# Conditioning chunks that hold a quarter of all four column blocks, and another order of the SSD outputs, in a hybrid decoder block

## The chip, the cores and the metric

The kernel runs on one core of one Trainium2 chip. The metric is the device time of one launch in microseconds (us), the median of three runs. One core has a matrix engine (PE, with its weight loads shown apart as PEld), three engines for elementwise work (DVE, ACT, POOL) and a queue of its own for transfers (SP); they run side by side, each in the order of its own instruction stream, and wait for one another through semaphores.

## The reference

One layer of a decoder for 256 prompt tokens and 8 samples of 4 tokens, 288 token columns in all. A conditioning vector per request (1 prompt + 8 samples, 9 columns) gives six modulation vectors of 2048; the layer is a modulated norm, one input projection shared by a pooling mixer and a Mamba-2 SSD mixer, one output projection, and a gated MLP with a short causal convolution.

```python
def block(x, c, st_pool, st_conv, st_ssm, st_ffn, pos0, lp):
    mod = silu(c) @ lp['w_ada'] + lp['b_ada']                 # 2048 -> 6 * 2048
    sh1, sc1, g1, sh2, sc2, g2 = split(mod, 6)
    h = rmsnorm(x, lp['norm1']) * (1 + sc1) + sh1
    u_pool, z, xbc, dt_raw = split(h @ lp['w_in'], [512, 2048, 4608])
    pool_out, new_pool = pool_mixer(u_pool, st_pool, pos0, lp['pool_w'], lp['pool_scale'])
    ssd_out, new_conv, new_ssm = ssd_mixer(z, xbc, dt_raw, st_conv, st_ssm, ...)
    x = x + g1 * (concatenate([pool_out, ssd_out]) @ lp['w_out'])
    h2 = rmsnorm(x, lp['norm2']) * (1 + sc2) + sh2
    gate, val = split(h2 @ lp['w_up'], 2)                     # 2 * 5504 wide
    gate_c, new_ffn = causal_dwconv(gate, st_ffn, ...)        # width 3
    return x + g2 * ((silu(gate_c) * val) @ lp['w_down'])

def ssd_chunked(xdt, dA, Bm, Cm, h0):                         # chunks of 128 tokens
    cs = cumsum(dA)
    y_diag = einsum(Cm, Bm, exp(cs_l - cs_s) masked, xdt)     # within a chunk
    y_off = einsum(Cm, h_start, exp(cs))                      # from the state at its start
    return y_diag + y_off, h_final
```

The last norm and the new states are outputs too. The six modulation vectors are the conditioning "parts" 0 to 5 (shift, scale and gate of the mixer, then of the MLP).

## The kernel before

Weights are streamed through SP's queue in chunks of 128 partitions by 1024 numbers (512 KB), by `load` (L209 to L212), into a pool of eight slots with the tag "raw"; a ninth is added in the output projection. A chunk of a projection is split by `split` into a rounded high part (ACT, L217) and the rest (DVE, L218), and each 128 x 128 block of it makes three matmuls with 288 columns (`mm3`, L223 to L225: high by high, high by low, low by high). They make up most of the work of PE. The matmuls on f32 operands, as the conditioning has them, leave two rows each in the trace.

Stages, in order of time: parts 0 and 1 of the conditioning in groups (`ada_group_units`, matmuls named adag), which gate the first modulation; the projection to x, B and C of the SSD mixer (xbc) and to its time steps (dt); the projections to z and to the pooling input (uz); the output projection (out, 16 blocks m); the second norm; the up projection in gate and value blocks (`up_pair`), the first three pairs with the weights upk in one sweep; the down projection and the last norm.

Parts 2 to 5 are not needed at once. `ada_part_units` (L312) makes one as a generator that other loops pull: it loads chunks, multiplies them, and yields after each visit. For a part there are 16 blocks k of 128 rows, and for each k two chunks h. Chunk h holds the column blocks j = 2h and 2h + 1 of the part, 512 columns each. `ada_mm` (L252) multiplies a chunk's block j with the stationary operand `sc_c[:, k, :]` (the nine conditioning columns after SiLU, padded to 32) and puts the result into rows 32j to 32j + 31 of one PSUM tile, so the four blocks use four column groups of the PE array. A visit is `AY` = 2 blocks k, so 4 chunks and 8 matmuls, in the order in which the chunks were loaded. When all k are in, ACT copies the tile (`asb`, L257), PE transposes it in four blocks of 128 columns (L263), and four additions on DVE (L327) put the result with the bias into `ada`.

Parts 2, 3 and 4 form one chain (`adas`). It is pulled in the last section of xbc (RA1), in the uz loop (RA2), once after it (TA) and after each block m of the output projection. Part 5 has visits of one k (default `ay=1`): GA = (2, 3), two before and three after the sums of the second norm (`final_sum`), and then two for each pair from the fourth on in `up_pair`'s loop.

The SSD mixer goes through four groups g of six heads, three turns t of two heads each. In a turn `decays(t)` broadcasts the cumulated log decays of two heads by a PE matmul each (cse, L682), ACT makes relu and exp (L687 to L689), DVE multiplies e by C·B (L690), and POOL multiplies ec by C (L691). One turn later `outputs(t)` makes the turn's ten matmuls: the samples' state part (yo by a selector, L700) and the samples' own (L703), 32 columns wide, the first prompt chunk (L706), and the second, which has a part from its own tokens (xdt1 by e, L709) and one from the state before it (s1 by ec, L710), 128 wide. Each has two row halves of 64, one for each head. The result goes to DVE, ACT (square) and POOL (sum of squares). All these stages are generators too, pulled between the matmuls of the uz loop (`pull(back, ...)`), as are those of the pooling mixer (`pool_units`, its matmul at L770).

The order on each engine is the compiler's: it cuts and interleaves the visits and the turns with the main stream of `mm3`.

Of the kernel before, what the change touches and what calls it, by code (L numbers as in the profile page):

```python
# [11 lines left out]
F32 = mybir.dt.float32  # L12
F32R = mybir.dt.float32r
AF = mybir.ActivationFunctionType
ALU = mybir.AluOpType
PSUM = bass.MemoryType.PSUM

P = 128
# [26 lines left out]
RA1, RA2, RB1, RB2, RB3 = 0.5, 0.4, 1.0, 1.0, 1.0  # L45
TA, ADA_OUT = 4, 4
TK = 4
GA = (2, 3)
XM = (0, 2, 5, 9)
SM0 = 10  # L50
YC = [(0, 1), (1, 1)] + [(m, 2) for m in range(2, KT, 2)]
# [80 lines left out]
def kernel(ctx: ExitStack, tc, ins, outs):  # L132
# [29 lines left out]
    ada = kp.tile([P, 6, KT, NC9], F32, name="ada")  # L162
    amul = kp.tile([P, 2, KT, NC9], F32, name="amul")
    bada = early[:, V_BADA:V_BADA + 96].rearrange("p (a k) -> p a k", a=6)
    sc_c = kp.tile([P, KT, 32], F32, name="sc_c")
    nc.vector.memset(sc_c, 0.0)
    nc.scalar.activation(sc_c[:, :, 0:NC9], ct, AF.Silu)

    wps = aux("warm")

# [37 lines left out]
    def load(key):  # L208
        off, cols = S.items[key]  # L209
        t = wp[0].tile([P, RAWC], F32, tag="raw", name="raw_" + "_".join(map(str, key)))  # L210
        nc.sync.dma_start(t[:, :cols], wflat[off:off + P * cols].rearrange("(p n) -> p n", p=P))
        return t  # L212
# [36 lines left out]
    def ada_mm(ps, raw, k, c0, nb, js):  # L249
        for j in js:  # L250
            c = c0 + (j - js[0]) * nb
            nc.tensor.matmul(ps[32 * j:32 * j + 32, :nb], sc_c[:, k, :], raw[:, c:c + nb],  # L252
                             start=(k == 0), stop=(k == KT - 1), tile_position=(0, 32 * j))

    def ada_sb(ps, nb, name, r=P):
# [16 lines left out]
    def ada_group_units(gi):  # L272

        k0, gk = KGROUPS[gi]
        nj = min(2 * gk, 4)
        nb = 2 * gk * P // nj
        per = RAWC // (nj * nb)
        ps = pa.tile([P, 512], F32, tag="ada", name=f"adag{gi}")
        for q in range(KT // per):
            raw = load(("ada", gi, q))  # L280
            yield
            if gk == 1:

                for kk in range(0, per, 2):
                    k = q * per + kk
                    for j in range(4):
                        nc.tensor.matmul(ps[32 * j:32 * j + 32, :nb], sc_c[:, k + j // 2, :],
                                         raw[:, kk * 256 + j * P:kk * 256 + j * P + P],
                                         start=(k == 0), stop=(k == KT - 2), tile_position=(0, 32 * j))
                if gi == 0 and q < WU[3]:  # L290
                    warm_pe(WU[2], raw[:, 0:P])
                continue
            for kk in range(per):
                ada_mm(ps, raw, q * per + kk, kk * nj * nb, nb, range(nj))
        r = 32 * nj
        if gk == 1:
            asb = ada_sb(ps, nb, f"g{gi}")
            pt = aux(f"adat_g{gi}")
            nc.tensor.matmul(pt[:, :r], asb[:, :nb], early[:, K_S2:K_S2 + r], start=True, stop=True)
            if gi == 0:  # L300
                warm_pe(WU[4], asb[:, 0:P])
        else:
            pt = ada_tr(ada_sb(ps, nb, f"g{gi}", r), nb, f"g{gi}", r)
        for i in range(nb // P):

            o = ada[:, 0:2, k0:k0 + gk, :].rearrange("p a (b i) c -> p a b i c", b=nj // 2)[:, :, :, i, :]
            b = bada[:, 0:2, k0:k0 + gk].rearrange("p a (b i) -> p a b i", b=nj // 2)[:, :, :, i]
            src = pt[:, i * r:(i + 1) * r].rearrange("p (a b c) -> p a b c", a=2, b=nj // 2)[:, :, :, 0:NC9]
            nc.vector.tensor_tensor(o, src, b.unsqueeze(3).to_broadcast([P, 2, nj // 2, NC9]), ALU.add)
        ada_scale(0, 1, early[:, V_N1:V_N1 + KT], k0, gk)  # L310

    def ada_part_units(part, ay=1):  # L312
        ps = pa.tile([P, 512], F32, tag="ada", name=f"adap{part}")
        for k in range(KT):
            raws = [load(("adap", part, k, h)) for h in range(2)]
            for h in range(2):
                ada_mm(ps, raws[h], k, 0, 512, range(2 * h, 2 * h + 2))
            if k % ay == ay - 1:
                yield
        asb = ada_sb(ps, 512, f"p{part}")  # L320
        yield
        pt = ada_tr(asb, 512, f"p{part}")
        for i in range(4):
            o = ada[:, part].rearrange("p (j i) c -> p j i c", j=4)[:, :, i, :]
            b = bada[:, part].rearrange("p (j i) -> p j i", j=4)[:, :, i]
            src = pt[:, i * P:(i + 1) * P].rearrange("p (j c) -> p j c", j=4)[:, :, 0:NC9]
            nc.vector.tensor_tensor(o, src, b.unsqueeze(2).to_broadcast([P, 4, NC9]), ALU.add)  # L327
        if part == 4:
            ada_scale(1, 4, vec[:, V_N2:V_N2 + KT], 0, KT)
        yield  # L330
# [56 lines left out]

    nc.scalar.activation(warm, sc_c[:, 0, 0:1], AF.Sqrt, scale=0.0)  # L390
    warm_pe(WU[0])
    ssum = aux("ssum1")
    for q in range(4):
# [12 lines left out]
    col_sums(ssum, sqs, early[:, K_S4:K_S4 + 1], True, True)  # L406
    rstd1p, rstd1 = rstd_of(ssum, D, "rstd1")

    cvp = [mx.tile([P, 5, CW], F32, tag="cvp", name=f"cvp{g}", bufs=4) for g in range(4)]

    def cvs(g):
# [189 lines left out]
    def ssd_group(g):  # L601
# [92 lines left out]
        def outputs(t, e, ec):  # L694
            assert (g, t) in zdone
            pq = aux(f"y{g}_{t}")
            rows = [slice(0, 64), slice(64, P)]
            for i, r in enumerate(rows):
                f = slice(64 * (2 * t + i), 64 * (2 * t + i) + 64)
                nc.tensor.matmul(pq[r, NP:N], yo[:, f], seli, start=True, stop=False)  # L700
            for i, r in enumerate(rows):
                f = slice(64 * (2 * t + i), 64 * (2 * t + i) + 64)
                nc.tensor.matmul(pq[r, NP:N], xdt[:, 2, f], e[:, i, NP:N], start=False, stop=True)  # L703
            for i, r in enumerate(rows):
                f = slice(64 * (2 * t + i), 64 * (2 * t + i) + 64)
                nc.tensor.matmul(pq[r, 0:P], xdt[:, 0, f], e[:, i, 0:P], start=True, stop=True)  # L706
            for i, r in enumerate(rows):
                f = slice(64 * (2 * t + i), 64 * (2 * t + i) + 64)
                nc.tensor.matmul(pq[r, P:NP], xdt[:, 1, f], e[:, i, P:NP], start=True, stop=False)  # L709
                nc.tensor.matmul(pq[r, P:NP], s1[:, f], ec[:, i, :], start=False, stop=True)  # L710
            yt = cf[:, t, 0:N]
            nc.vector.scalar_tensor_tensor(out=yt, in0=yt,
                                           scalar=vec[:, V_D + 3 * g + t:V_D + 3 * g + t + 1],
                                           in1=pq[:, :N], op0=ALU.mult, op1=ALU.add)
            zt = zy[g][:, t, :]
            nc.vector.tensor_tensor(zt, zt, yt, ALU.mult)
            sq = kp.tile([P, N], F32, tag="xsq", name=f"ysq{g}_{t}", bufs=2)
            nc.scalar.activation(sq, zt, AF.Square)
            if g + t == 0:
                nc.gpsimd.tensor_copy(ssq, sq)  # L720
            else:
                nc.gpsimd.tensor_tensor(ssq, ssq, sq, ALU.add)
# [249 lines left out]
            drain(adas)  # L972


    adag2 = ada_part_units(5)
    for k in range(2):
        ready[("upk", k)] = split(load(("upk", k)), 0, 2 * FK * P, f"upk{k}")
    for _ in range(GA[0]):
# [102 lines left out]
    for gi, (k0, nk) in enumerate(DGROUPS):  # L1081
        for j in range(k0, k0 + nk):
            up_pair(j)
            if gi == 0 and j >= 3:
                next(adag2, None)
                next(adag2, None)
            if j >= SM0:
                next(states, None)
            if gi and j == k0:
                drain(adag2)  # L1090
                down(gi - 1)
# [32 lines left out]
def _layout(inp):  # L1124
# [62 lines left out]
    for key in _STREAM.order:  # L1187
        o, cols = _STREAM.items[key]
        kind = key[0]
        if kind == "ada":  # L1190
            k0, gk = KGROUPS[key[1]]
            per = RAWC // (256 * gk)
            s = wa[key[2] * per:(key[2] + 1) * per, :, 0:2, k0:k0 + gk]
            s = s.transpose(1, 0, 2, 3, 4)
        elif kind == "dt":
            s = wdt.transpose(1, 0, 2)
        elif kind == "adap":
            s = wa[key[2], :, key[1], 8 * key[3]:8 * key[3] + 8]
        elif kind == "xbc":
            ks, ms = _xbc_chunks(key[1])[key[2]]  # L1200
            s = wx[ks][:, :, ms].transpose(1, 2, 0, 3)
        elif kind == "upk":
            s = wu[key[1]][:, [m for j in range(FK) for m in (j, FT + j)]]
        elif kind == "down":
            k0, nk = DGROUPS[key[1]]
            a, n = _halves(nk)[key[3]]
            s = wd[k0 + a:k0 + a + n, :, key[2]].transpose(1, 0, 2)
        else:
            mat, m0 = full[kind]
            a, n = _halves(KT)[key[-1]]  # L1210
            s = mat[a:a + n, :, m0 + key[1]].transpose(1, 0, 2)
        w[o:o + P * cols] = s.reshape(-1)
# [47 lines left out]
```

## Time and profile before

| | us |
|---|---|
| runs | 1397.7, 1397.77, 1396.01; median 1397.7 |
| profiled execution, its own time | 1395.98 |
| its span | 1394.2 |
| mean granted clock of PE | 0.997 |
| DMA, mean rate over the span | 232 GB/s |

The span is the time from the first to the last instruction of the profiled execution; its own time holds what lies around that as well. In a row of the timeline stand the start, the length, the engine, the line, the operation with its output and inputs, and how many rows it stands for; a bracket gives the idle time before it and what ended it. For matmuls the ends are modelled, and they overlap, so what a run of them takes is read from its start to the start of what follows. In a group's row the busy time and the mean of one row in nanoseconds follow the bar. Line numbers are those of the kernel before.

### The profile page before, as it was taken

To read this page: it belongs to the slowest core of one execution; us is meant where nothing else is said; L and a number is where in the kernel's file an instruction comes from. 1 tells how busy PE (TensorE), PEld (TensorE's weight loads), DVE (VectorE), ACT (ScalarE), POOL (GpSimd) and SP (SyncE) were. 2 spreads that over 40 slices of the span, in tenths; PEclk is the share of its full clock that TensorE was granted. 3 is DMA by queue.
4 is the path that set the end of the run, shared out by engine and by line. 5 is a ranking of instruction groups with operands and counts; after the bars stand their busy time and mean duration, and the time that the engine had idled before them with its cause. 6 is when DMAs were issued, how large, how long until landed. Compare 5 with 4: busy or idle time off the path is not lost.

```text
span 1394.2 us, 26416 instructions
## 1 busy us (share of the span) xinstructions
PE 1374.9 (99%) x10565; PEld 1253.5 (90%) x10565; DVE 822.3 (59%) x1409; ACT 577.0 (41%) x925; POOL 259.8 (19%) x466
## 2 busy tenths in 40 slices
PE   8999999999999999999999999999999999999997
PEld 7777888776668998989999999999999999999997
DVE  3775666867465446845665445666664466666553
ACT  5322333466673334533443333444343344444452
POOL 0000000344332222211211000221220011122221
PEclk9999999999999999999999999999999999999999
DMA  8889886867869886688655555655555555555631
GB/s 339 313 318 316 294 287 248 338 248 289 321 228 354 319 313 244 215 287 296 210 185 181 164 172 181 207 184 186 176 180 169 180 190 189 192 188 193 194 118 68
DMA packets 97196, 323.20 MB, mean 232 GB/s; under 512 B 10737, under 2 KB 19889, under 8 KB 97073
## 3 DMA queue, kind: packets, MB, share of 16 engines
q1 hardware_dynamic: 93168, 310.63, 64.8%
q0 software_dynamic: 3184, 9.69, 2.0%
q8 instruction: 83, 1.36, 0.4%
q10 hardware_dynamic: 720, 1.19, 0.2%
q14 instruction: 41, 0.33, 0.1%
HBM read 309.78 MB, written 10.39 MB: 230 GB/s over the span
## 4 chain that ended last, share of the span: by engine, by line
PE 70%; DVE 1%; issue 0%; ACT 0%; POOL 0%; DVEq 0%; POOLq 0%; ACTq 0%
PE mm_down L223 7%; PE mm_down L225 7%; PE mm_down L224 7%; PE mm_gate L225 6%; PE mm_gate L223 6%; PE mm_val L224 6%; PE mm_gate L224 6%; PE mm_val L225 6%; PE mm_val L223 6%; PE mm_out L223 3%; PE mm_out L224 2%; PE mm_out L225 2%; PE adap L252 2%; PE mm_up L223 1%; PE mm_up L224 1%; PE mm_up L225 1%
## 5 line engine op out<-in xcount | busy, mean ns | idle before, releaser
L223 PE MATMUL mm_down<-ah,whi_down 128*128 128x288 f32 x688 | 203.7, 296 | 0.0
L225 PE MATMUL mm_down<-ah,wlo_down 128*128 128x288 f32 x688 | 203.5, 296 | 0.0
L224 PE MATMUL mm_down<-al,whi_down 128*128 128x288 f32 x688 | 203.3, 295 | 0.0
L225 PE MATMUL mm_gate<-h2h,wlo_gate 128*128 128x288 f32 x640 | 190.2, 297 | 0.0
L223 PE MATMUL mm_gate<-h2h,whi_gate 128*128 128x288 f32 x640 | 189.8, 297 | 0.0
L224 PE MATMUL mm_gate<-h2l,whi_gate 128*128 128x288 f32 x640 | 189.3, 296 | 0.0
L224 PE MATMUL mm_val<-h2l,whi_val 128*128 128x288 f32 x640 | 188.8, 295 | 0.0
L225 PE MATMUL mm_val<-h2h,wlo_val 128*128 128x288 f32 x640 | 188.5, 295 | 0.0
L223 PE MATMUL mm_val<-h2h,whi_val 128*128 128x288 f32 x640 | 188.0, 294 | 0.0
L218 DVE TENSOR_TENSOR wlo_gate<-raw_gate,whi_gate 128x1024 fp32r<-128x1024 f32 x80 | 98.4, 1232 | 140.5 <-ACT whi_gate L217 140.3
L218 DVE TENSOR_TENSOR wlo_down<-raw_down,whi_down 128x1024 fp32r<-128x1024 f32 x96 | 108.2, 1127 | 116.0 <-ACT whi_down L217 115.1
L217 ACT CAST whi_down<-raw_down 128x1024 fp32r<-128x1024 f32 x96 | 92.2, 961 | 168.8 <-PE mm_down L224 120.3
L217 ACT CAST whi_gate<-raw_gate 128x1024 fp32r<-128x1024 f32 x80 | 83.8, 1050 | 168.3 <-PE mm_gate L224 76.2
L223 PE MATMUL xbc<-h1h,whi_xbc 128*128 128x288 f32 x448 | 139.1, 312 | 2.4 <-ACT h1h L350 1.3
L217 ACT CAST whi_val<-raw_val 128x1024 fp32r<-128x1024 f32 x80 | 84.1, 1051 | 127.8 <-issue 101.0
L224 PE MATMUL xbc<-h1l,whi_xbc 128*128 128x288 f32 x448 | 132.2, 296 | 0.0
L225 PE MATMUL xbc<-h1h,wlo_xbc 128*128 128x288 f32 x448 | 130.5, 298 | 0.6 <-DVE wlo_xbc L218 0.5
L224 PEld LDWEIGHTS mm_down<-al,whi_down 128*128 128x128 f32 x688 | 129.7, 189 | 0.0
L225 PEld LDWEIGHTS mm_down<-ah,wlo_down 128*128 128x128 f32 x688 | 129.6, 188 | 0.0
L223 PEld LDWEIGHTS mm_down<-ah,whi_down 128*128 128x128 f32 x688 | 129.6, 188 | 0.0
L223 PEld LDWEIGHTS mm_gate<-h2h,whi_gate 128*128 128x128 f32 x640 | 120.4, 188 | 5.0 <-ACT ah L1025 4.2
L224 PEld LDWEIGHTS mm_gate<-h2l,whi_gate 128*128 128x128 f32 x640 | 120.6, 189 | 0.0
(321 smaller groups left out, 3043.1 us busy)
## 6 DMA issues: line engine op xcount, KB each, us to landing
raw_adap<-wflat SPq DMA_DIRECT2D x128, 512.0 KB, 4.9
raw_gate<-wflat SPq DMA_DIRECT2D x80, 512.0 KB, 3.7
raw_val<-wflat SPq DMA_DIRECT2D x80, 512.0 KB, 3.5
raw_ada<-wflat SPq DMA_DIRECT2D x64, 512.0 KB, 5.5
raw_xbc<-wflat SPq DMA_DIRECT2D x55, 512.0 KB, 5.9
raw_down<-wflat SPq DMA_DIRECT2D x48, 512.0 KB, 3.6
raw_out<-wflat SPq DMA_DIRECT2D x32, 512.0 KB, 7.0
raw_down<-wflat SPq DMA_DIRECT2D x32, 384.0 KB, 3.1
```

The source lines that it names most:

```text
L217: nc.scalar.copy(hi[:, :n], raw[:, a:a + n])
L218: nc.vector.tensor_tensor(lo[:, :n], raw[:, a:a + n], hi[:, :n].bitcast(F32), ALU.subtract)
L223: nc.tensor.matmul(ps, whi[:, w], bh, start=first, stop=False)
L224: nc.tensor.matmul(ps, whi[:, w], bl, start=False, stop=False)
L225: nc.tensor.matmul(ps, wlo[:, w], bh, start=False, stop=last)
L252: nc.tensor.matmul(ps[32 * j:32 * j + 32, :nb], sc_c[:, k, :], raw[:, c:c + nb], start=(k == 0), stop=(k == KT - 1), tile_position=(0, 32 ...
```

## The change

A conditioning chunk of parts 2 to 5 holds other columns: chunk h of block k has, of all four column blocks j, the 256 columns that belong to h (the host lays the weights out so). `sc_c` gets a second copy, with the nine columns at 16 to 24, that serves h = 1: both chunks then go into the same 256 columns of PSUM, h = 0 into rows 0 to 8 and h = 1 into rows 16 to 24 of each block of 32. A visit issues all its loads first, then its matmuls from the last chunk to the first, 16 of 256 columns for two k. The tile is 256 wide, so there are two transposes and two additions for a part. Part 5 has visits of two k as well (GA = (1, 2), then one visit for a pair). `outputs` begins with the state part of the second chunk (s1 by ec) and ends with the samples, each kind of matmul for both row halves in turn.

```diff
-GA = (2, 3)
+GA = (1, 2)
...
-    sc_c = kp.tile([P, KT, 32], F32, name="sc_c")
+    sc_c = kp.tile([P, 2, KT, 32], F32, name="sc_c")
     nc.vector.memset(sc_c, 0.0)
-    nc.scalar.activation(sc_c[:, :, 0:NC9], ct, AF.Silu)
+    nc.scalar.activation(sc_c[:, 0, :, 0:NC9], ct, AF.Silu)
...
     def ada_part_units(part, ay=1):
         ps = pa.tile([P, 512], F32, tag="ada", name=f"adap{part}")
-        for k in range(KT):
-            raws = [load(("adap", part, k, h)) for h in range(2)]
-            for h in range(2):
-                ada_mm(ps, raws[h], k, 0, 512, range(2 * h, 2 * h + 2))
-            if k % ay == ay - 1:
-                yield
-        asb = ada_sb(ps, 512, f"p{part}")
-        yield
-        pt = ada_tr(asb, 512, f"p{part}")
-        for i in range(4):
-            o = ada[:, part].rearrange("p (j i) c -> p j i c", j=4)[:, :, i, :]
-            b = bada[:, part].rearrange("p (j i) -> p j i", j=4)[:, :, i]
-            src = pt[:, i * P:(i + 1) * P].rearrange("p (j c) -> p j c", j=4)[:, :, 0:NC9]
-            nc.vector.tensor_tensor(o, src, b.unsqueeze(2).to_broadcast([P, 4, NC9]), ALU.add)
+        for k0 in range(0, KT, ay):
+            todo = [(k, h, load(("adap", part, k, h))) for k in range(k0, k0 + ay) for h in range(2)]
+            for k, h, raw in reversed(todo):
+                for j in range(4):
+                    nc.tensor.matmul(ps[32 * j:32 * j + 32, :256], sc_c[:, h, k, :], raw[:, 256 * j:256 * j + 256],
+                                     start=(k == ay - 1 and h == 1), stop=(k == KT - ay and h == 0),
+                                     tile_position=(0, 32 * j))
+            yield
+        asb = ada_sb(ps, 256, f"p{part}")
+        yield
+        pt = ada_tr(asb, 256, f"p{part}")
+        for i in range(2):
+            o = ada[:, part].rearrange("p (m i) c -> p m i c", i=2)[:, :, i, :]
+            b = bada[:, part].rearrange("p (m i) -> p m i", i=2)[:, :, i]
+            src = pt[:, i * P:(i + 1) * P].rearrange("p (m c) -> p m c", m=8)[:, :, 0:NC9]
+            nc.vector.tensor_tensor(o, src, b.unsqueeze(2).to_broadcast([P, 8, NC9]), ALU.add)
...
+    nc.gpsimd.tensor_copy(sc_c[:, 1, :, 16:16 + NC9], sc_c[:, 0, :, 0:NC9])
...
         def outputs(t, e, ec):
-            rows = [slice(0, 64), slice(64, P)]
-            for i, r in enumerate(rows):
-                f = slice(64 * (2 * t + i), 64 * (2 * t + i) + 64)
+            halves = [(i, slice(64 * i, 64 * i + 64), slice(64 * (2 * t + i), 64 * (2 * t + i) + 64))
+                      for i in range(2)]
+            for i, r, f in halves:
+                nc.tensor.matmul(pq[r, P:NP], s1[:, f], ec[:, i, :], start=True, stop=False)
+            for i, r, f in halves:
+                nc.tensor.matmul(pq[r, P:NP], xdt[:, 1, f], e[:, i, P:NP], start=False, stop=True)
+            for i, r, f in halves:
+                nc.tensor.matmul(pq[r, 0:P], xdt[:, 0, f], e[:, i, 0:P], start=True, stop=True)
+            for i, r, f in halves:
                 nc.tensor.matmul(pq[r, NP:N], yo[:, f], seli, start=True, stop=False)
-            for i, r in enumerate(rows):
-                f = slice(64 * (2 * t + i), 64 * (2 * t + i) + 64)
+            for i, r, f in halves:
                 nc.tensor.matmul(pq[r, NP:N], xdt[:, 2, f], e[:, i, NP:N], start=False, stop=True)
-            for i, r in enumerate(rows):
-                f = slice(64 * (2 * t + i), 64 * (2 * t + i) + 64)
-                nc.tensor.matmul(pq[r, 0:P], xdt[:, 0, f], e[:, i, 0:P], start=True, stop=True)
-            for i, r in enumerate(rows):
-                f = slice(64 * (2 * t + i), 64 * (2 * t + i) + 64)
-                nc.tensor.matmul(pq[r, P:NP], xdt[:, 1, f], e[:, i, P:NP], start=True, stop=False)
-                nc.tensor.matmul(pq[r, P:NP], s1[:, f], ec[:, i, :], start=False, stop=True)
...
-    adag2 = ada_part_units(5)
+    adag2 = ada_part_units(5, AY)
...
             if gi == 0 and j >= 3:
                 next(adag2, None)
-                next(adag2, None)
...
         elif kind == "adap":
-            s = wa[key[2], :, key[1], 8 * key[3]:8 * key[3] + 8]
+            s = wa[key[2], :, key[1]].reshape(P, 4, 2, 2 * P)[:, :, key[3]]
```

More of the change, by code (lines that the diff above doesn't have):

```diff
@@ L251, in ada_mm @@
             c = c0 + (j - js[0]) * nb
-            nc.tensor.matmul(ps[32 * j:32 * j + 32, :nb], sc_c[:, k, :], raw[:, c:c + nb],
+            nc.tensor.matmul(ps[32 * j:32 * j + 32, :nb], sc_c[:, 0, k, :], raw[:, c:c + nb],
                              start=(k == 0), stop=(k == KT - 1), tile_position=(0, 32 * j))
@@ L286, in ada_group_units @@
                     for j in range(4):
-                        nc.tensor.matmul(ps[32 * j:32 * j + 32, :nb], sc_c[:, k + j // 2, :],
+                        nc.tensor.matmul(ps[32 * j:32 * j + 32, :nb], sc_c[:, 0, k + j // 2, :],
                                          raw[:, kk * 256 + j * P:kk * 256 + j * P + P],
@@ L386, in xav @@
         return xa[k0 // 4][:, k0 % 4:k0 % 4 + gk, :]
-    nc.scalar.activation(warm, sc_c[:, 0, 0:1], AF.Sqrt, scale=0.0)
+    nc.scalar.activation(warm, sc_c[:, 0, 0, 0:1], AF.Sqrt, scale=0.0)
     warm_pe(WU[0])
```

## The prediction, made before the changed kernel ran

> **What bounds the kernel now.** I read the page's first part, then the busy time of each engine by stretches, then PE's waits.
>
> ```profile
> span 1394.2 us, 26416 instructions
> PE 1374.9 (99%) x10565; PEld 1253.5 (90%) x10565; DVE 822.3 (59%) x1409; ACT 577.0 (41%) x925; POOL 259.8 (19%) x466
> ```
> ```profile
> 222.00:300.00 78.00, 76.99 (x582) 57.79 (x581) 57.50 (x128) 38.45 (x71) 21.04 (x36) 1.00 0.85 320
> ...
> 312.00:317.00 5.00, 2.14 (x15) 1.70 (x13) 5.00 (x11) 4.97 (x11) 2.24 (x4) 0.98 0.40 111
> 317.00:321.00 4.00, 4.00 (x21) 3.66 (x22) 3.33 (x10) 3.97 (x12) 1.29 (x3) 0.59 1.04 388
> ...
> 540.00:666.00 126.00, 126.00 (x952) 117.06 (x952) 80.90 (x133) 56.90 (x94) 26.48 (x54) 1.00 0.79 268
> 666.00:1394.00 728.00, 718.72 (x5402) 718.19 (x5398) 417.21 (x607) 286.12 (x406) 124.25 (x253) 1.00 0.55 177
> ```
> ```profile
> PE mm_uz L225 <- DVE wlo_uz L218: 1.4, 1, 1.4
> PE cse L682 <- DVE ada L327: 1.4, 1, 1.4
> ...
> PE xbc L223 <- ACT whi_xbc L217: 0.9, 1, 0.9
> ...
> PE y L703 <- DVE e L690: 0.4, 1, 0.4
> ...
> PE pool L770 <- DVE pout L765: 0.2, 1, 0.2
> ```
>
> PE is busy for 99% of the span. From 540 us to the output's tail it has no gap worth naming, so whatever PE saves or loses earlier reaches the end, and a microsecond of PE issue is a microsecond of time unless a wait takes its place. The columns of a stretch are its length, then PE, PEld, DVE, ACT, POOL, the clock, the DMA share. Only 312 to 321 is not PE's: there DVE is busy 5.00 of 5.00, PE 2.14, and the next 4.00 us of PE run at a clock of 0.59. Every edit of the change lies before 666 us.
>
> **The visits' issue.** The conditioning matmuls are the group to be changed; the second group has the new shape already.
>
> ```profile
> L252 PE MATMUL adap<-raw_adap,sc_c 128*32 128x512 f32 x512 | 75.8, 600 | 0.0
> ...
> L252 PE MATMUL adag<-raw_ada,sc_c 128*32 128x256 f32 x384 | 33.7, 390 | 0.0
> ```
> ```profile
> 96.09 1.07 PE L252 MATMUL adag<-raw_ada,sc_c 128*32 128x256 f32 x16
> 97.09 0.41 PE L223 MATMUL xbc<-h1h,whi_xbc 128*128 128x288 f32 x1
> ...
> 107.59 0.64 PE L252 MATMUL adag<-raw_ada,sc_c 128*32 128x256 f32 x8
> 108.16 0.40 PE L223 MATMUL xbc<-h1h,whi_xbc 128*128 128x288 f32 x1
> ```
> ```profile
> 391.51 1.05 PE L252 MATMUL adap<-raw_adap,sc_c 128*32 128x512 f32 x2
> 392.49 0.31 PE L700 MATMUL y<-vec,yo 128*64 128x32 f32 x4
> 392.73 1.07 PE L252 MATMUL adap<-raw_adap,sc_c 128*32 128x512 f32 x8
> 393.72 0.31 PE L703 MATMUL y<-e,xdt 128*64 128x32 f32 x4
> 393.86 0.42 PE L706 MATMUL y<-e,xdt 128*64 128x128 f32 x4
> 394.11 0.44 PE L709 MATMUL y<-e,xdt 128*64 128x128 f32 x4
> 394.33 0.44 PE L710 MATMUL y<-ec,s 128*64 128x128 f32 x4
> ```
> ```profile
> 409.04 0.29 PE L225 MATMUL mm_uz<-h1h,wlo_uz 128*128 128x288 f32 x1
> 409.27 1.92 PE L252 MATMUL adap<-raw_adap,sc_c 128*32 128x512 f32 x16
> 411.12 0.40 PE L223 MATMUL mm_out<-mixh,whi_out 128*128 128x288 f32 x1
> 411.45 1.04 PE L252 MATMUL adap<-raw_adap,sc_c 128*32 128x512 f32 x2
> ```
>
> A matmul of f32 makes two rows, so the run at 409.27 is eight matmuls of 512 columns, one full visit. It takes 411.12 − 409.27 = 1.85, the run of eight rows 393.72 − 392.73 = 0.99: four column blocks side by side cost a round of 0.86, and 0.13 is fixed. At 391.51 a single matmul takes 0.98: a round with one block filled costs a whole round. At 256 columns, 1.00 for sixteen rows and 0.57 for eight give a round of 0.43 and 0.14 fixed. A full visit is thus worth the same, 0.14 + 4 × 0.43 = 1.86 against 1.85: the new shape as such gains nothing. What differs is how the compiler cuts the visits. In its order for the kernel before, 256 matmuls stand in 48 stretches, which make 76 rounds of 512 where 64 would do; in that for the changed one, 512 stand in 44 stretches, 137 rounds of 256 where 128 would do. Issue: 76 × 0.86 = 65.2 becomes 137 × 0.43 = 59.2, **−6.0**. A matmul between two runs (411.12 to 411.45) takes 0.33, where a step of the main stream is 0.13; with the fixed 0.14 a stretch costs 0.34, and four fewer give **−1.3**. Eight transposes fewer, by the 0.25 that two f32 matmuls 128 wide take at 393.86, give **−1.0**.
>
> [...]
>
> ```profile
> L252 PEld LDWEIGHTS adap<-raw_adap,sc_c x32: 106/108/109, 321.6 to 329.8; 128*32 128x32 f32 x32
> ```
> One such load takes 0.108 (the middle of the three).
>
> **SSD outputs.** They stand in 24 stretches before and 22 after: usually two matmuls and then eight, and only 3 of 12 turns become one run. The change does here a quarter of what its words say. Two fewer stretches, 0.7, and some pairing of s1·ec with xdt1·e, which 394.11 and 394.33 bound at 0 to 0.6: **−1.0**. But s1·ec now comes first, and needs POOL's product.
>
> ```profile
> 286.69 0.43 PE L682 MATMUL cse<-csr,selr 128*128 128x288 f32 x2
> ...
> 287.84 1.28 ACT L688 ACT_TABLE_LOAD   x1
> ...
> 290.36 0.73 POOL L691 TENSOR_TENSOR ec<-ec,cf 128x256 f32<-128x256 f32 x1 [7.42 <-ACT ec L688]
> ```
>
> In group 0 the decays of the first turn end on POOL at 291.09, 4.4 after the first cse row. In the changed order 24 steps of 0.13, four cse matmuls and the entry stand between, 3.8: PE waits 0.6. Group 3 has the same turn (0.6), one turn each of groups 0 and 2 lacks 0.5 and 0.3 by the same count, and e is late by 0.2 in one: **+2.1** (1.0 if ACT and POOL move up with PE, 2.3 at most). Behind it in PE's order stand the visit and the main stream. The removed late e (0.4) is not counted: its cut visit is replaced by another.
>
> **Visits begin with the last chunk.** The four loads of a visit go out on SP's queue in order, and the one issued last is now needed first.
>
> ```profile
> 324.62 0.82 SPq L211 DMA_DIRECT2D raw_adap<-wflat  x2
> ...
> 410.36 0.80 SPq L211 DMA_DIRECT2D raw_adap<-wflat  x2
> ```
> ```profile
> 328.86 1.98 PE L252 MATMUL adap<-raw_adap,sc_c 128*32 128x512 f32 x8
> ```
> ```profile
> DMA to landing us min/median/max: 3.6/7.3/9.5
> ```
>
> In part 3 the second visit's last chunk already comes just in time: the run at 328.86 takes 1.98 where eight rows take 1.07, 0.9 of waiting inside it. Its slot is freed by a read of the visit before, which the reversal makes late; from there only about 2.4 of PE work is left, against 0.4 for the issue (half of the 0.82 row) and at least 3.6 to the landing, and it shares the queue with the chunk before it (512 KB at the 388 GB/s that the stretch from 317 shows take 1.4, of which I add half): 4.7 − 2.4, **+2.3** (0 to 3.6). Part 4's second visit has the same pair at 410.36: its later chunk was wanted last, and is wanted first; there I take 1.5. Behind it stands the pool matmul (0.2 of waiting now), which comes sooner after it, 0.9 more: **+2.4** (0 to 3.0). In the 32 visits the others have room: loads go out several us before the visit. In 222 to 300, with the DMA engines at 0.85 and PE once held 0.9 by an xbc load, what part 2 saves before 275 (about 1.0 of the issue) is mostly not passed on: **+0.8** (0 to 1.0).
>
> **312 to 321 us.** PE idles 5.00 − 2.14 = 2.9 there and then loses 4.00 × 0.41 = 1.6 to the clock. e of group 1 is ready when DVE is done, about 320. In the changed order about 17 us of PE work, no longer 18.3, stand before it, and DVE has two adds fewer to make. What is given back is a wait that starts later, and less of the work runs at half clock: **−1.4** (−2.1 to +0.5).
>
> **Around the second norm.**
>
> ```profile
> 537.20 2.77 PE L252 MATMUL adap<-raw_adap,sc_c 128*32 128x512 f32 x22
> ...
> 539.01 0.43 ACT L350 CAST h2h<-h_n 128x288 fp32r<-128x288 f32 x1 [1.31 <-POOL h_n L348]
> ...
> 539.90 0.53 PE L223 MATMUL mm_up<-h2h,whi_upk 128*128 128x288 f32 x2
> ```
>
> The run of 22 rows covers the time until h2h is ready at 539.44, and passes it by 0.46. The changed order has a shorter run of three rounds of 256, 1.4 with its fixed part, ending 538.7: its gain is in the issue already, of which **+0.8** goes to a wait (0 to 0.85). Part 5's one visit for each gate pair lies in a stretch with PE at 126.00 of 126.00, and its loads keep their number. The second copy of sc_c on POOL, long before any chunk, and the larger memset are costed at nothing; uncovered, either would be well under 1 us, by POOL's 0.73 for a wider product.
>
> **Sum.** −6.0 − 1.3 − 1.0 − 1.0 + 2.1 + 2.3 + 2.4 + 0.8 − 1.4 + 0.8 = −2.3. The profiled execution's own time is 1395.98, so 1393.7; it lies 1.7 under the median of 1397.7, and the same step from there gives **1395.4**. About 0.2% (2.8 us) is what a measurement can tell from no change.
>
> **Rivals.**
> A, the waits don't come: engines ahead of PE move up with it, and loads go out as slots free earlier. Then −9.3 with the −1.4 left out: 1397.7 − 9.3 = 1388.4. For it: DVE, ACT and POOL are at 59% and less. Against it: the 1.98 run shows a chunk that was late already.
> B, the waits cost all of it. The two visits' waits of over 2 us leave PE idle and the clock falls, as after the idle stretch at 312; one such window costs 1.6, two 3.2: −2.3 + 3.2, about 1398.6. For it: that clock row. Against: those waits are shorter than the 2.9 there.
> C, slower: the order of chunks. Chunks in a busy stretch land about 1.4 apart (512 KB at 388 GB/s), and each visit now needs its last. Where a visit has less room, it pays up to that. From four visits beyond the two counted it costs 5.6 and decides (−2.3 + 5.6, 1401.0); with six it is 1403.8. For it: the DMA share of 0.85, and SP waits for slots. Against: in the kernel before only one visit of this kind shows a wait.
> D, weight loads exposed: 128 passes by the 0.108 of a load would be +13.8 and leave 1409.2. Against it stand the rows at 96.09 and 107.59. [...]
>
> **Chances.** The forecast's case 0.50 (its own range 1392.5 to 1398.5), A 0.17, B 0.18, C 0.13, D 0.02. Faster by over 0.2% means under 1394.9: A, and nearly half of the first, 0.40. Same, up to 1400.5: the other half and most of B, 0.40. Slower 0.20: C, D and the upper part of B. The range from 1389.0 to 1401.0 leaves out C's far end, D and half of A.
>
> **What would show it.** The adap group at 256 columns, x1024, busy time near 1024 × 0.39 by overlap, but its stretches' sum near 59 + 6; a run of 16 rows at 1.0 and of 32 at 1.9; s1·ec waits for POOL's ec of 0.3 to 0.6 in four turns; an adap wait near 2 in each of parts 3 and 4; a wait for h2h under 1. If a run of 32 rows took well over 1.9, D would hold; adap waits in many visits would show C, and none A.

## The result and the profile after

The changed kernel takes 1404.5 us (median of 4 runs, 1404.0 to 1406.0) against 1397.7 (4 runs): ratio 1.0054, with a 95% interval of 1.0041 to 1.0068. It is slower by about 7 us, where 2.3 us faster was forecast, and outside the range. The page's first lines, the group of the conditioning matmuls by shape, and PE's waits, each with its total, how often, and the longest:

```profile
span 1402.2 us, 27382 instructions
...
PE 1370.4 (98%) x11069; PEld 1270.6 (91%) x11069; DVE 821.8 (59%) x1401; ACT 575.6 (41%) x925; POOL 254.9 (18%) x467
```
```profile
L321 PE MATMUL adap<-raw_adap,sc_c 128*32 128x256 f32 x1024 | 69.8, 388 | 4.5 <-DMA raw_adap<-wflat 4.5
```
```profile
PE adap L321 <- DMA raw_adap<-wflat: 4.5, 1, 4.5
PE mm_uz L225 <- DVE wlo_uz L218: 2.7, 2, 1.7
PE y L706 <- POOL ec L697: 2.6, 3, 1.4
PE mm_out L224 <- DVE mixl L914: 2.0, 1, 2.0
...
PE cse L688 <- DVE ada L332: 1.3, 1, 1.3
...
PE pool L774 <- DVE pout L769: 1.2, 1, 1.2
...
PE mm_up L223 <- ACT h2h L355: 0.8, 1, 0.8
```

PE is busy for 4.5 us less, and the span is 8.0 longer. One wait of 4.5 for a conditioning load stands first in the list; in the kernel before no load held PE for as much as 1.

Where the time went can be read from the main stream: the matmuls of lines L223 to L225 come in nearly the same sequence in every kernel here (8736 of them, at most 103 at another place), so the start of the n-th is a milestone. The table has the start in the kernel before, and for the others how much later the same matmul starts (negative: earlier), in us; n = 1500 lies in the uz projection before part 3 begins, 1770 at its end, 1915 nearly three blocks into the output projection, 2530 at its end, 2580 in the up sweep, 3450 after part 5. The other columns belong to the experiments below. Each column is one profiled execution; that of e2 is the fastest of its runs, 2.7 under their median, the others lie within 1.8 of theirs.

| n | before | changed | e1 | e10 | e9 | e5 | e3 | e2 | e4 |
|---|---|---|---|---|---|---|---|---|---|
| 1500 | 319.4 | −2.3 | −2.3 | −2.7 | −2.2 | −2.5 | −2.8 | −2.6 | −2.3 |
| 1570 | 342.0 | +6.5 | +5.0 | +4.2 | +5.9 | −0.5 | −1.5 | −0.8 | −1.8 |
| 1770 | 408.4 | +4.8 | +4.5 | +3.1 | +5.0 | −2.2 | −2.4 | −3.8 | −5.1 |
| 1915 | 435.9 | +7.7 | +8.9 | +6.1 | +5.1 | +0.8 | +1.6 | −3.7 | −5.0 |
| 2530 | 530.2 | +7.6 | +8.8 | +6.0 | +5.1 | +0.7 | +1.5 | −3.7 | −5.1 |
| 2580 | 544.8 | +9.3 | +10.4 | +7.7 | +6.7 | +2.4 | +3.1 | −2.9 | −4.3 |
| 3450 | 671.8 | +8.2 | +9.4 | +6.6 | +5.6 | +1.3 | +2.0 | −4.0 | −5.4 |
| span | 1394.2 | +8.0 | +9.2 | +6.4 | +5.4 | +1.2 | +1.9 | −4.2 | −5.6 |

The changed kernel gains 2.3 up to n = 1500. Then it loses 8.8 between 319 and 342, where the second visit of part 3 lies, and 2.9 at the start of the output projection; the rest is small. The first place, in the timelines of PE and of SP's queue (start, length, operation, rows; in brackets the idle time before and what ended it), with the time from issue to landing of the conditioning loads from 320 to 333 behind them:

```profile
321.08 1.05 PE L321 MATMUL adap<-raw_adap,sc_c 128*32 128x256 f32 x10
322.06 0.40 PE L688 MATMUL cse<-csr,selr 128*128 128x288 f32 x1
322.38 1.50 PE L321 MATMUL adap<-raw_adap,sc_c 128*32 128x256 f32 x22
323.81 0.44 PE L706 MATMUL y<-ec,s 128*64 128x128 f32 x4
...
324.60 0.29 PE L714 MATMUL y<-e,xdt 128*64 128x32 f32 x4
329.41 1.06 PE L321 MATMUL adap<-raw_adap,sc_c 128*32 128x256 f32 x2 [4.52 <-DMA raw_adap<-wflat]
...
335.10 1.94 PE L321 MATMUL adap<-raw_adap,sc_c 128*32 128x256 f32 x16
```
```profile
321.78 1.63 SPq L211 DMA_DIRECT2D raw_adap<-wflat  x2
```
```profile
DMA to landing us min/median/max: 3.5/6.3/7.9
```

The second visit begins at 329.41 with the chunk that was loaded last. Its load is the second of the pair at 321.78: the two issues lie 1.28 apart (1.63 less one issue's 0.35), because the first visit, which frees the slots, is cut by a cse matmul at 322.06. It goes out at about 323.06 and takes 6.3 us, the middle of the three, to land; PE has work for it to hide behind only until 324.9. Sixteen rows that take 1.0 elsewhere need 1.9 at 335.10, where the granted clock was 0.50. The stretches of the changed kernel (length, then PE, PEld, DVE, ACT, POOL, granted clock, DMA share, GB/s), and below them the whole region in the changed kernel and in the kernel before:

```profile
325.00:329.40 4.40, 0.00 (x0) 0.00 (x0) 1.58 (x3) 3.63 (x4) 0.79 (x1) 0.92 0.85 299
329.40:338.80 9.40, 9.39 (x49) 5.56 (x50) 2.62 (x4) 2.18 (x4) 2.39 (x6) 0.50 0.20 75
```
```profile
309.00:344.00 35.00, 27.47 (x210) 20.07 (x209) 19.67 (x36) 20.97 (x46) 10.32 (x16) 0.80 0.52 179
```
```profile
309.00:344.00 35.00, 32.14 (x248) 22.93 (x240) 26.47 (x45) 22.86 (x48) 18.48 (x25) 0.95 0.70 251
```

After the empty 4.4 us PE ran 9.4 us at a clock of 0.50, which is 4.7 us of work lost, more than the wait itself. Over the region PE is idle for 7.5 against 2.9, and its busy time ran at 0.80 against 0.95 (27.47 × 0.20 = 5.5 against 32.14 × 0.05 = 1.6): 8.5 more in all, nearly the whole 8.8.

### The profile page after: what moved, and what is told of

Read it like the earlier page. It is cut to its first block, busy times and chain, and to the rows that moved or that the text cites. A ratio compares the mean times of both kernels' runs of the same rounds, so it can differ in the third digit from the quotient of the medians.

```text
span 1402.2 us, 27382 instructions
## 1 busy us (share of the span) xinstructions
PE 1370.4 (98%) x11069; PEld 1270.6 (91%) x11069; DVE 821.8 (59%) x1401; ACT 575.6 (41%) x925; POOL 254.9 (18%) x467
## 4 chain that ended last, share of the span: by engine, by line
PE 69%; DVE 1%; ACT 0%; issue 0%; POOL 0%; DVEq 0%; POOLq 0%; ACTq 0%
PE mm_down L223 7%; PE mm_down L225 7%; PE mm_down L224 7%; PE mm_gate L225 6%; PE mm_gate L223 6%; PE mm_val L224 6%; PE mm_gate L224 6%; PE mm_val L225 6%; PE mm_val L223 6%; PE mm_out L223 3%; PE mm_out L224 2%; PE mm_out L225 2%; PE adap L321 2%; PE mm_up L223 1%; PE mm_up L225 1%; PE mm_up L224 1%
## 5 line engine op out<-in xcount | busy, mean ns | idle before, releaser
L223 PE MATMUL mm_down<-ah,whi_down 128*128 128x288 f32 x688 | 203.7, 296 | 0.0
L225 PE MATMUL mm_down<-ah,wlo_down 128*128 128x288 f32 x688 | 203.5, 296 | 0.0
L225 PE MATMUL mm_gate<-h2h,wlo_gate 128*128 128x288 f32 x640 | 190.3, 297 | 0.0
L223 PE MATMUL mm_gate<-h2h,whi_gate 128*128 128x288 f32 x640 | 189.8, 296 | 0.0
L225 PE MATMUL mm_val<-h2h,wlo_val 128*128 128x288 f32 x640 | 188.5, 295 | 0.0
L223 PE MATMUL mm_val<-h2h,whi_val 128*128 128x288 f32 x640 | 188.0, 294 | 0.0
L223 PE MATMUL xbc<-h1h,whi_xbc 128*128 128x288 f32 x448 | 139.2, 312 | 1.9 <-ACT h1h L355 1.3
L225 PE MATMUL xbc<-h1h,wlo_xbc 128*128 128x288 f32 x448 | 130.3, 298 | 0.7 <-DVE wlo_xbc L218 0.7
L225 PEld LDWEIGHTS mm_down<-ah,wlo_down 128*128 128x128 f32 x688 | 129.6, 188 | 0.0
L223 PEld LDWEIGHTS mm_down<-ah,whi_down 128*128 128x128 f32 x688 | 129.6, 188 | 0.0
L223 PEld LDWEIGHTS mm_gate<-h2h,whi_gate 128*128 128x128 f32 x640 | 120.5, 188 | 2.1 <-ACT ah L1029 1.6
```

What stands on the lines that cost most here:

```text
L223: nc.tensor.matmul(ps, whi[:, w], bh, start=first, stop=False)
L225: nc.tensor.matmul(ps, wlo[:, w], bh, start=False, stop=last)
```

## The experiments

Three theories were on record: (1) the chunk that is loaded last and wanted first makes the wait, and the half clock behind it; (2) the new order of the SSD outputs is what costs; (3) the quarter chunks cost in every visit. Ratios are against the kernel before on the same chip, with 95% intervals.

**e1, one visit turned back.** The second visit of part 3 in the order of loading:

```diff
-            for k, h, raw in reversed(todo):
+            for k, h, raw in (todo if (part, k0) == (3, ay) else reversed(todo)):
```

> As the changed kernel (1404.5), but the second visit of part 3 takes its chunks in the order of loading. Theory 1 (the chunk loaded last, wanted first, makes the 4.5 us wait there and the half clock behind it): the adap wait falls below 1.5, the stretch from 317 to 342 loses 6 to 9 us, 1396 to 1398.5. Theory 2 (the SSD outputs' new order, with its waits for ec, is what costs): 1403 to 1405. Theory 3 (the quarter chunks themselves cost, in every visit): 1403 to 1405.

Measured: 1405.1 (5 runs, 1400.3 to 1405.9), ratio 1.0047 (1.0031 to 1.0063). Theory 1 in this narrow form failed. PE's timeline of e1, and a stretch ahead of it and one behind it:

```profile
326.31 0.62 PE L321 MATMUL adap<-raw_adap,sc_c 128*32 128x256 f32 x2 [0.17 <-DMA raw_adap<-wflat]
...
330.35 0.62 PE L321 MATMUL adap<-raw_adap,sc_c 128*32 128x256 f32 x2 [2.06 <-DMA raw_adap<-wflat]
```
```profile
317.00:321.00 4.00, 4.00 (x20) 3.12 (x18) 2.11 (x7) 2.36 (x7) 0.81 (x1) 0.51 0.81 288
...
331.00:338.00 7.00, 7.00 (x39) 4.88 (x40) 2.62 (x4) 1.83 (x4) 0.97 (x3) 0.51 0.92 341
```

The wait falls from 4.5 to 2.2, but the same load still comes at 330.3 and is wanted before then in any order; and the clock was at 0.51 already from 317 on, and again for 7 us behind the wait of 2.06. Its runs fall in two groups, 1400.3 and 1401.5, and 1405.1 to 1405.9; the profiled one is of the second.

**e2, all visits turned back.**

```diff
-            for k, h, raw in reversed(todo):
+            for k, h, raw in todo:
...
-                                     start=(k == ay - 1 and h == 1), stop=(k == KT - ay and h == 0),
+                                     start=(k == 0 and h == 0), stop=(k == KT - 1 and h == 1),
```

> As the changed kernel, but every visit takes its chunks in the order of loading, quarter chunks and the new SSD order kept. Theory 1: as the run with one visit turned back, and the part of the loss at the start of the output projection (2.9) may go too: 1393 to 1398. Theory 2: 1403 to 1405. Theory 3: 1403 to 1405.

Measured: 1394.5 (8 runs, 1391.8 to 1395.6), ratio 0.9981 (0.9971 to 0.9992). 10 us come back, in the table at 319 to 342 and at 408 to 436 above all. Most of the loss hangs on the reversal.

**e3, the SSD outputs as before**, with quarter chunks and reversal kept (the body of `outputs` taken from the kernel before).

> As the changed kernel, but the SSD outputs in the order of before. Theory 1: only the waits for ec (2.6) come back, and the 4.5 us wait stays: 1402 to 1404. Theory 2: 1395 to 1398. Theory 3: 1402 to 1404.

Measured: 1397.0 (10 runs), ratio 1.0002 (0.9992 to 1.0011). By the expectation this spoke for theory 2, but together with e2 it says that in this region the two parts need each other: either of them undone removes most of the 8.8. Over the whole kernel they come nearer to adding up: against e4 below, which has neither (1390.4), the reversal costs 6.7, the SSD order 4.1, and both 14.1. PE and SP in e3 at the same place:

```profile
321.40 1.07 PE L321 MATMUL adap<-raw_adap,sc_c 128*32 128x256 f32 x16
322.74 1.06 PE L321 MATMUL adap<-raw_adap,sc_c 128*32 128x256 f32 x14
326.91 1.48 PE L321 MATMUL adap<-raw_adap,sc_c 128*32 128x256 f32 x18 [1.22 <-DMA raw_adap<-wflat]
```
```profile
322.09 0.82 SPq L211 DMA_DIRECT2D raw_adap<-wflat  x2
```

Without the cse matmul inside a chunk's run the pair of loads goes out 0.4 apart, the second lands at 326.9, and the wait is 1.2, with the clock at 1.00 behind it (329 to 333); e3 loses 1.3 over this region.

**e4, quarter chunks alone**, visits as in e2 and SSD outputs as in e3.

> Quarter chunks alone: visits in the order of loading and the SSD outputs in the order of before. Theory 1: the issue saving is left with little against it, 1390 to 1395. Theory 2: 1390 to 1395 as well. Theory 3: 1400 or more.

Measured: 1390.4 (1389.7 to 1390.7), ratio 0.9952 (0.9937 to 0.9967). Theory 3 falls: the chunks gain 6.7 us (1397.1 − 1390.4).

**e5, the load left out.** In the changed kernel the last chunk of part 3's second visit isn't loaded, and the chunk of the block before it is read again in its place (part 3 lacks that chunk's product and has another twice):

```diff
-            todo = [(k, h, load(("adap", part, k, h))) for k in range(k0, k0 + ay) for h in range(2)]
+            todo = []
+            for k in range(k0, k0 + ay):
+                for h in range(2):
+                    same = (part, k, h) == (3, 2 * ay - 1, 1)
+                    todo.append((k, h, todo[-2][2] if same else load(("adap", part, k, h))))
```

> As the changed kernel, but the last chunk of the second visit of part 3 is not loaded: its matmuls read the chunk of the block before it again (part 3, the shift of the MLP, is then wrong by that chunk). Theory 1 (that one load, late by the turnaround of its slot, makes the 4.5 us wait and the half clock behind it): the stretch from 317 to 342 loses at most 3 instead of 8.8, the time is 1396 to 1399. Rival (the waits for ec and the order of the SSD outputs would stall PE there anyway, as in the run that turned this visit back): 1402 to 1405.

Measured: 1397.8 (10 runs), ratio 1.0007 (0.9997 to 1.0016). 6.7 of the 7 us are gone with one load, although reversal and SSD order stay. The region from 309 to 344 in e5:

```profile
309.00:344.00 35.00, 29.93 (x280) 23.24 (x279) 24.72 (x44) 22.98 (x48) 15.40 (x20) 0.95 0.63 221
```

The clock is back to 0.95. PE still idles for 5.1: waits for wlo_uz (3.1 in two) and for ec take the place, and this region still costs 2.1 (−2.5 to −0.5 in the table). The queue itself is no faster: the load of raw_uz that now stands in that place, issued 1.29 behind the first, takes 6.5 to land. What is gone is a visit that cannot start without it.

**e6, the SSD order alone**, in the kernel before (only `outputs` changed).

> The kernel before with the new order of the SSD outputs alone. If waits for ec cost by themselves what they cost beside forward quarter chunks (1394.5 against 1390.4): 1400 to 1403. If they cost only where loads are late as well: 1397 to 1398.

Measured: 1398.9 (10 runs, 1397.3 to 1402.7), ratio 1.0013 (1.0004 to 1.0023): +1.9, between the two expectations. It costs by itself, and about 4 beside forward quarter chunks (e2 against e4).

**e7, the reversal alone**, in the kernel before: four loads, then the eight matmuls of 512 columns from the last chunk on.

```diff
-        for k in range(KT):
-            raws = [load(("adap", part, k, h)) for h in range(2)]
-            for h in range(2):
-                ada_mm(ps, raws[h], k, 0, 512, range(2 * h, 2 * h + 2))
-            if k % ay == ay - 1:
-                yield
+        for k0 in range(0, KT, ay):
+            todo = [(k, h, load(("adap", part, k, h))) for k in range(k0, k0 + ay) for h in range(2)]
+            for k, h, raw in reversed(todo):
+                for j in range(2):
+                    q = 2 * h + j
+                    nc.tensor.matmul(ps[32 * q:32 * q + 32, :512], sc_c[:, k, :], raw[:, 512 * j:512 * j + 512],
+                                     start=(k == ay - 1), stop=(k == KT - ay), tile_position=(0, 32 * q))
+            yield
```

> The kernel before with its visits loaded as a whole and taken from the last chunk to the first (512-column chunks, old SSD order). If the reversal costs what it costs beside quarter chunks and the old SSD order (1397.0 against 1390.4): 1402 to 1406. If it costs only with quarter chunks: 1396 to 1399.

Measured: 1404.9, ratio 1.0055 (1.0040 to 1.0070). Without quarter chunks and without the new SSD order the reversal does as much harm as the whole change. It does so at the same two places: e7 is 0.2 ahead at n = 1500, 5.9 behind at 1570 and 8.9 at 1915. Here too a cse matmul cuts the first visit (at 325.41), the pair of loads goes out 1.31 apart, and the second takes 5.3 to land. PE's waits in e7:

```profile
PE mm_uz L225 <- DVE wlo_uz L218: 3.4, 2, 2.0
PE adap L319 <- DMA raw_adap<-wflat: 3.4, 2, 2.7
```

**e8, a paired tail.** As e4, but the last four SSD matmuls of a turn as s1 by ec for both halves, then xdt1 by e for both:

```diff
             for i, r in enumerate(rows):
                 f = slice(64 * (2 * t + i), 64 * (2 * t + i) + 64)
+                nc.tensor.matmul(pq[r, P:NP], s1[:, f], ec[:, i, :], start=True, stop=False)
+            for i, r in enumerate(rows):
+                f = slice(64 * (2 * t + i), 64 * (2 * t + i) + 64)
-                nc.tensor.matmul(pq[r, P:NP], xdt[:, 1, f], e[:, i, P:NP], start=True, stop=False)
-                nc.tensor.matmul(pq[r, P:NP], s1[:, f], ec[:, i, :], start=False, stop=True)
+                nc.tensor.matmul(pq[r, P:NP], xdt[:, 1, f], e[:, i, P:NP], start=False, stop=True)
```

> Quarter chunks with visits in the order of loading, the SSD outputs in the order of before except the last four matmuls, s1 by ec for both halves and then xdt1 by e for both. If the pairing of the row halves is worth what I took for it (0.05 for each of 12 turns) and no wait comes of it: 1389.5 to 1390.5, against 1390.4 without.

Measured: 1389.8 (1389.4 to 1391.1), ratio 0.9952 (0.9936 to 0.9969). It lies 0.6 under e4 by the medians, inside the spread of either. This or e4 is the version to keep; both beat the kernel before.

**e9, the second visit of part 4 turned back** (as e1's edit, with `(part, k0) == (4, ay)`).

> As the changed kernel, but the second visit of part 4, at the start of the output projection, takes its chunks in the order of loading; nothing else of PE's order differs. If the 2.9 us that are lost from 408 to 436 come of a visit that cannot begin before its last chunk has landed: the wait for mixl (2.0) is covered and 2.5 to 3.5 come back, 1401 to 1402. If mixl is late for another reason: 1404 to 1405.

Measured: 1401.4, ratio 1.0032 (1.0019 to 1.0045). 3.1 come back, all of it between n = 1770 and 1915 (+0.1 instead of +2.9). Timelines of PE at this place, in the changed kernel and in e9:

```profile
417.52 0.75 PE L774 MATMUL pool<-pout,poolw 128*128 128x288 f32 x2 [1.20 <-DVE pout L769]
...
420.44 0.40 PE L224 MATMUL mm_out<-mixl,whi_out 128*128 128x288 f32 x1 [1.95 <-DVE mixl L914]
...
421.11 1.06 PE L321 MATMUL adap<-raw_adap,sc_c 128*32 128x256 f32 x2
```
```profile
417.77 0.75 PE L774 MATMUL pool<-pout,poolw 128*128 128x288 f32 x2 [1.20 <-DVE pout L769]
418.67 1.50 PE L321 MATMUL adap<-raw_adap,sc_c 128*32 128x256 f32 x24
420.70 0.41 PE L224 MATMUL mm_out<-mixl,whi_out 128*128 128x288 f32 x1 [0.53 <-DVE mixl L914]
```

DVE brings mixl at nearly the same time in both. In the order of loading three chunks of the visit (24 rows) are there to fill the time until then. Reversed, the visit cannot begin before its last chunk has landed, at 419.6, and in the compiler's order it stands behind the matmul that wants mixl, so nothing fills it. The clock has a part here too; the stretch behind the wait, in the changed kernel and in e9:

```profile
421.00:424.00 3.00, 3.00 (x9) 1.80 (x9) 1.81 (x5) 0.00 (x0) 0.00 (x0) 0.50 0.97 371
```
```profile
421.00:424.00 3.00, 3.00 (x19) 2.32 (x18) 2.89 (x9) 0.44 (x1) 0.00 (x0) 1.00 1.01 369
```

Of the 3.1 that come back, the shorter wait is 1.4 (1.95 to 0.53) and the clock 1.5 (3.00 × 0.50).

**e10, the first two visits of part 3 turned back** (`fwd = part == 3 and k0 <= ay`, with the start flag to match).

> As the changed kernel, but the first two visits of part 3 take their chunks in the order of loading. If it was the first visit's reversal that frees the slot of the wanted chunk late (why turning back the second alone did not help): the adap wait falls below 1.5, 1396 to 1399. If the load is late whatever the order, and the waits for ec bring the loss: 1402 to 1405.

Measured: 1402.4 (9 runs, 1398.9 to 1404.7), ratio 1.0037 (1.0025 to 1.0048): −2.1, inside the second expectation, with an adap wait of 2.0. PE's order from 309 up to the second visit is that of e2, yet e2 passes the region with +1.8 and e10 with +6.9. What differs first is the clock. Two stretches of e2, then the same of e10:

```profile
315.00:317.00 2.00, 1.23 (x9) 1.26 (x10) 2.00 (x7) 1.98 (x6) 0.00 (x1) 1.00 0.95 340
317.00:321.00 4.00, 3.38 (x37) 2.60 (x39) 3.04 (x9) 2.89 (x7) 0.82 (x1) 1.00 1.01 363
```
```profile
315.00:317.00 2.00, 2.00 (x9) 2.00 (x10) 2.00 (x6) 2.00 (x5) 0.00 (x0) 0.50 0.95 318
317.00:321.00 4.00, 4.00 (x20) 3.12 (x21) 1.74 (x6) 1.97 (x7) 0.84 (x1) 0.51 0.72 258
```

Both had the same two waits before (1.7 for wlo_uz and 1.3 for ada); after them one execution went on at a clock of 1.00 and the other at 0.50. The later visits' loads then went out at other times: the late one landed 4.9 us after its issue in e2, where other transfers were still under way (DMA share 0.79 from 321 to 323), and 6.1 in e10, where none were (0.00). Behind its wait of 1.95 e10 went to half clock once more, 0.50 from 331.2 to 334.6. So e1 and e10 also carry what the clock did before the visit, and one trace of each cannot separate the two.

## Why the prediction was wrong

Its step that failed is the term for part 3's second visit: "4.7 − 2.4, +2.3 (0 to 3.6)". The place and the mechanism were named, a slot freed late and a chunk wanted first; its landing was taken too short, the work left too long, and the clock behind the wait was not in it. The wait came to 4.5, over the upper end of 3.6.

- The landing. It was taken as 0.4 + 3.6 + 0.7 = 4.7 from the release of the slot; the load took 6.3. The sum took the minimum of the row 3.6/7.3/9.5, which is the first load of a pair. For the second of the pair as it stood in the kernel before, 4.7 was right: issued at 325.07, it took 4.7 to land. What the sum did not see is that in the changed order the second load goes out 1.28 behind the first, where it was 0.45. The work left was 2.4 by the count and is 1.8 (323.06 to 324.9), so PE waited 4.5.
- The clock. The sum charged the wait alone. The row 329.40 to 338.80 at 0.50 adds 4.7. Rival B had this mechanism, for both visits, and it came at both: 4.7 here and 1.5 at 421 to 424. B charged 1.6 for each, from the 4 us at 0.59 in the kernel before, and held the waits too short for it. Yet the clock was at 0.50 from 328.7 to 339.0 with the wait of 4.5 (changed kernel, 324.9 to 329.4), from 330.8 to 337.7 behind that of 4.1 (e9), from 331.2 to 338.0 behind a single wait of 2.06 (e1) and from 331.2 to 334.6 behind one of 1.95 (e10). And in nine of ten traces (the kernel before, the changed one, e1, e3 to e5, e7, e9 and e10, but not e2) it was at 0.50 within or behind two waits of 1.1 to 1.7 each, at 310 to 317. No run here shows what decides whether it falls.

Of the 10.3 us between the forecast step (−2.3) and the span's (+8.0), the longer wait is 2.2 and the clock behind it 4.7.

e5 settles that the two hang on that load: without it 6.7 come back, and the clock with them. e2 and e7 settle that the reversal brings it about (−10 when it is undone, +7.9 alone). How the SSD order adds to it is argued from the traces and was not tried by itself: beside quarter chunks it brings a cse matmul into the first visit's reading, which sets the two issues 1.28 apart; without the cut they lie 0.4 apart and the wait is 1.2 (e3). e7 has such a cut without the SSD order. The gap alone does not decide: e2 has it too (1.29) and loses little. How much of the 8.8 a kept clock would have saved was not tried either; 4.7 is by the rows.

The other terms:

- Issue, −9.3 in all with its SSD part: quarter chunks alone gain 6.7. In e4's order 47 stretches stand in place of 44 and the SSD's −1.0 is absent; with these two left out, and the terms for DMA, DVE and h2h kept, the sum was −6.0 − 0.3 − 1.0 + 0.8 − 1.4 + 0.8 = −7.1. The −1.4 in it did not come in e4 either (2.2 ahead at n = 1485, 2.0 at 1510), so that −7.1 lies so near 6.7 is in part luck. The reading of full and half-filled rounds held: e4's order has 137 rounds again, and its visits' stretches, each from its start to the start of what follows and without idle gaps, sum to 65.8 against 72.6 in the kernel before (0.9 of it the waiting inside the run at 328.86), which is 5.9 to 6.8 less where the sum had 6.0 + 0.3. Rival D, whose 128 passes are the 512 rows more in four column blocks side by side, is out: runs of 32 rows take 1.87 (414.05 to 415.92 in the changed kernel) where 1.86 was predicted and exposed loads would add to it.
- SSD order, +2.1 − 1.0 = +1.1: too small. It costs 1.9 by itself (e6) and 4.1 beside forward quarter chunks (e2 against e4); the changed kernel has ec waits of 2.6 in three turns.
- Part 4's second visit, +2.4: 2.9 in the table, 3.1 in e9. Right in size by luck: what it loses is cover for mixl (1.4) and the clock behind that (1.5), where the sum had the visit's own landing and a wait for the pool matmul.
- h2h, +0.8: 0.8. The up sweep shows +1.7 because one more block k of part 5 stands ahead of it (six, not five), of which 1.1 comes back by n = 3450.
- 312 to 321, −1.4: it did not come. The changed kernel is 1.8 ahead at n = 1485 (312.3 in the kernel before), 2.2 at 1505 (320.4) and 1.5 at 1510 (321.2). The waits for wlo_uz and ada are there as before (1.7 and 1.3), and so is half clock behind them (0.51 from 315.0 to 318.5, in the kernel before 0.54 from 317.0 to 320.5).
- Rival C needed four more late visits. One wait is in the list; no others came.

## What to carry to other kernels

A consumer that takes a batch of loads from the last to the first starts when the last has landed and gives up the cover that the earlier ones were; where slots are recycled just in time, take them in the order of loading. Price a load by its place in its queue, not by the minimum of the stretch, which here was the first load of a pair (3.6 before and 3.5 after, where the second took 4.7 and 6.3), and ask whether the change moves the time at which its slot comes free. Add to a PE wait the clock that may follow it: here 4.7 us behind a wait of 4.5, and 1.5 behind one of 1.95. Undo the parts of a change in pairs: here each of two parts undone alone gave back 7 us or more, and what the third gained showed only without the two.

## What the runs showed of the hardware beyond that

One and the same order of work on PE, with the same two waits of 1.7 and 1.3 us, went with a clock of 1.00 throughout in one execution (e2) and of 0.50 for 6.8 us in another (e10). The other traces of the ten show 0.50 there for 3.4 us (the kernel before, the changed one, e4, e5) or for 6.8 (e1, e3, e7, e9). Runs of one kernel spread unequally, e10 from 1398.9 to 1404.7 and e4 from 1389.7 to 1390.7, though e4 has the same two waits and a clock of 0.50 for 3.4 us; the reason was not tried.

The second of two 512 KB loads that were issued onto a nearly idle queue (DMA share 0.00 from 321 to 322 in the changed kernel, and from 320.0 to 323.0 in e3) landed 4.3 us after its issue where the issues lay 0.4 apart (e3), and 5.3 to 6.3 where they lay 1.3 apart (changed kernel, e1, e7, e9, e10). In the changed kernel the DMA engines were at 0.85 and moved 299 GB/s from 325.00 to 329.40, which is 1.3 MB, two and a half such loads: two more had gone out 0.4 and 0.9 us behind it. That alone does not explain it, since in the kernel before the second of two loads 0.45 apart, issued at 325.07 with more behind it from 325.94 on, took 4.7. Why the wider gap goes with a later landing was not tried.
